# Modulation blocks of layer two at the layer border, first pair's loads ahead of the last down blocks, and another tensor estimate in the interleaving

## The chip, the cores and the metric

One core of a Trainium2 chip runs the whole program. The metric is device time in microseconds (us), the median of three runs. A profiled execution gives the span of the instructions and the trace.

## The reference

One inference step of a two-layer backbone over 640 tokens (128 prompt tokens and 512 sample tokens that use the same weights), width 1024, in float32. Cut to what matters here, a layer is

```
shift1, scale1, gate1, shift2, scale2, gate2 = split(silu(cond) @ w_ada[l] + b_ada[l], 6)   # one vector per group
h = rms_norm(x) * (1 + scale1) + shift1
z = h @ w_in                     # conv streams, q, k, v, state-space input u, three branch gates
merged = sum of three gated branches (conv, attention, bidirectional state space), each through its own projection
x += gate1 * (merged @ w_out)
h = rms_norm(x) * (1 + scale2) + shift2
x += gate2 * ((silu(h @ w_ffn_gate) * (h @ w_ffn_up)) @ w_ffn_down)      # inner width 2816
```

## The kernel before

**Products.** The residual x lives in eight tiles of 128 features by 640 tokens. A float32 product is made of three products of rounded halves (high by high, high by low, low by high), each over 2 x 320 columns; one weight block of 128 output features over 8 feature tiles is 48 products of 320 columns. The feed-forward part (L1966 on) has three plain blocks m = 0, 1, 2 (a gate block and an up block each) and then pairs: from m = 3 a gate and an up block are made together by a scheme of seven products in place of eight (`glu_pair`, L901, 84 products of 320 columns). `sums` (L860) makes the combined activations for it. The 22 inner blocks come in five parts of 4, 4, 4, 5 and 5; each part ends in eight down blocks (m = 0 to 7) that add into x. The part's last block lets the norm of the next stage begin.

**Weights.** `order` lists all weight blocks in the order of their use. `w_fill` (L385) issues the loads in this order on SP's queue into three raw slots (`wr`); a pair takes one `wr` slot and two `pt` tiles, and two of its parts are summed in flight by a second transfer that POOL issues with an add. `converter` (L429) is a side job that turns each raw block into a rounded high half (ScalarE cast) and a low half (VectorE subtraction), up to two blocks ahead of the one in use (`may`, L417). Modulation blocks pass by the converter: `w_get` (L482) takes them raw.

**Modulation.** w_ada is used in blocks of 512 x 256 (512 KB), four products each. `ada_n` (L319) says after which weight block how many modulation blocks come: in the first layer one after every pair (m = 3 to 21), one after most projection blocks, and so on. Those in the gaps are loaded by `ada_pre` (L670) into ordinary `c` tiles and multiplied by `ada_fill` (L682). The norm of the feed-forward part fills its waits with them (`FILL2` = 0, 5, 5: so many ahead of the last statistics product, ahead of and behind the broadcast product in `rstd` and `norm_rows`, L731 to L760). At the border from layer one to two the counts `FILL1` are 0, 0, 0. `ada_flush` starts a side job that turns finished sums into the vectors (`ada_rows`).

**Order of the work.** All engine queues are in order, and the program writes them by an interleaving planner. The main stream (weight blocks) yields what it needs next; `pump` (L534) then steps side jobs (converter, sums, state space, attention) whose next step is due, by a running estimate of each engine's time (`Clock`, `Engine`), no later than the main stream's. The estimate of a product is at L142: (columns + 32) / 2.4 ns, so 146.7 ns for 320 columns; a VectorE operation on 640 columns is taken as 737 ns. `clk.calm` keeps state-space and attention jobs back; it is set for the last two down blocks of layer one and taken back in `norm`. `cvt.hold` keeps the converter from being stepped in pairs, where `advance` steps it by hand. The state-space side jobs of layer two start ahead of the last eight down blocks of layer one (`ssm_begin`).

Of the kernel before, what the change touches and what calls it, by code (L numbers as in the profile page):

```python
# [17 lines left out]
KD = D // 128  # L18
FF = 2816
KF = FF // 128  # L20
DEPTH = 2
# [8 lines left out]
SLACK = 0  # L30
ADA0 = 2
GO = 0
FILL1 = (0, 0, 0)
FILL2 = (0, 5, 5)
GN, GF = sum(FILL2), sum(FILL1)
CV = 0
# [76 lines left out]
class Engine:  # L113
# [5 lines left out]
    def __getattr__(self, op):  # L119
        f, key, clock = getattr(self.eng, op), self.key, self.clock  # L120

        def is_ap(x):
            return hasattr(x, "partition_size")

        def size(x):
            n = 1
            for d in x.shape[1:]:
                n *= d
            return n

        def call(*args, **kw):
            res = f(*args, **kw)  # L132
            out = kw.get("out", args[0] if args else None)
            ins = [x for x in list(args[1:] if "out" not in kw else args) +
                   [v for k, v in kw.items() if k not in ("out", "accum_out")] if is_ap(x)]
            outs = [out.name] + ([kw["accum_out"].name] if "accum_out" in kw else [])
            n = max([size(out)] + [size(x) for x in ins]) if key != "pe" else size(out)
            if key == "pe":
                if op == "transpose":
                    cost = 2 * n / 2.4  # L140
                elif ins[-1].dtype == F32R:
                    cost = (max(n, 256) + 32) / 2.4  # L142
                else:
                    cost = 4 * n / 2.4
                    if out.shape[0] == 32:
                        cost /= 3
            elif key == "act":
                cost = 100 + n / 1.2 + (90 if "accum_out" in kw else 0)
            elif key == "dve":
                one = op in ("tensor_scalar", "tensor_copy", "memset") and all(x.space == out.space for x in ins)  # L150
                cost = 70 + n / (1.6 if one else 0.96)
            else:
                s = max([clock.t["pe"] if key == "dma" else clock.t[key]] + [clock.avail.get(x, 0.0) for x in outs] +
                        [clock.w.get(x.name, 0.0) for x in ins])
                if key == "pool":
                    clock.t[key] = e = s + 1000
                else:
                    clock.issue = max(clock.issue, s) + 475.0
                    rate = 180.0 if min(x.shape[-1] for x in [out] + ins) < 128 else 360.0
                    clock.t[key] = e = max(clock.t[key], clock.issue) + 4 * n * out.shape[0] / rate  # L160
                for x in outs:
                    clock.w[x], clock.by[x] = e + 2000, "dma"
                return res
            clock.op(key, cost, outs, [x.name for x in ins])
            return res
        return call
# [3 lines left out]
def trunk_kernel(ctx: ExitStack, tc: tile.TileContext, a):  # L170
    nc = tc.nc
    clk = Clock()
# [18 lines left out]

    def bps():
        while clk.slot("m") >= clk.HELD:
            min((x for x in sides if not x.busy and not x.hold), key=lambda x: x.time()).step()
        t = psb.tile([128, 2, 512], F32, tag="b", name="bps")
        clk.ring("b", t.name, 4)
        return t
# [121 lines left out]
    def ada_n(key):  # L319

        nm, l, m = key
        if nm == "pa":
            return 1 + int(m == 0)
        if nm == "fgu":
            return int(l == 0)
        if nm == "fd":
            return int(l == 0 and m in (4, 8))
        return int(nm == "o" and m < 7 - GO or l == 0 and (nm in ("cc", "cb") or nm == "fg" and m > 1))
# [50 lines left out]
        ada_gap(GF)  # L379
    assert not ada_o  # L380

    wst = {"load": 0, "use": 0, "made": 0, "used": 0, "over": 0, "pair": 0, "wr": 0, "pt": 0}
    wraw, wtile = {}, {}

    def w_fill():  # L385

        while wst["load"] < len(order):
            key, srcs, nr, ncol = order[wst["load"]]
            part = key[3] if key[0] == "fgu" else 0
            if not part and (wst["wr"] == WR or key[0] == "fgu" and wst["pt"] == 2):  # L390
                return
            if part:
                t = f32(ptp.tile([128, 2, TK], F32R, tag="pt", name="pt").rearrange("p a b -> p (a b)"))
            else:
                t = wrp.tile([128, 1024], F32, tag="wr", name="wr")
                clk.ring("wr", t.name, WR)
                wst["wr"] += 1
                wst["pt"] += int(key[0] == "fgu")
            rows = lambda o, x: (t[:, o:o + x.shape[0] // 128 * ncol].rearrange("p (k m) -> p k m", m=ncol),
                                 x.rearrange("(k p) m -> p k m", p=128))  # L400
            for o, x, y in srcs:
                sp.dma_start(*rows(o, x))
                if y is not None:
                    pool.dma_start(*rows(o, y), accum_op=OP.add)
            wraw[key] = t
            wst["load"] += 1
# [22 lines left out]
    def converter():  # L429
        u = -1  # L430
        raws = []

        def put(hl):
            nonlocal u
            u += 1
            while units[u][0] == "ada":
                u += 1
            wtile[u] = [hl[r].rearrange("p (k m) -> p k m", m=ncol) for r in range(2)]

        for i, (key, srcs, nr, ncol) in enumerate(order):  # L440
            if key[0] == "ada":
                continue
            yield lambda: key in wraw
            raws.append(wraw.pop(key))
            if key[0] == "fgu":
                if key[3] == 2:
                    for hl in pair_units(u + 1, *raws):
                        if not isinstance(hl, list):
                            yield hl
                            continue  # L450
                        put(hl)
                    raws = []
                    w_free("pt")
            else:
                yield may
                put((yield from halves(raws.pop(), nr * ncol)))
                w_free("wr")
# [24 lines left out]
    def w_get(key):  # L482
        u = wst["use"]
        assert units[u] == key, (units[u], key)
        wst["use"] += 1
        if key[0] == "ada":
            return wraw.pop(key)[:, 0:1024].rearrange("p (k m) -> p k m", k=4)
        wst["used"] += 1 - wst["over"]
        wst["over"] = int(key[0] == "fgu" and key[3] == 3)
        while u not in wtile:  # L490
            cvt.step()
        return wtile.pop(u)
# [15 lines left out]
    class Side:  # L508
# [1 line left out]


        def __init__(self, gen, prio):
            self.gen, self.prio, self.done, self.busy, self.hold = gen, prio, False, False, False
            sides.append(self)
            sides.sort(key=lambda x: x.prio)
            self.step()
# [17 lines left out]
    def pump(need=(), until=None):  # L534
# [3 lines left out]
        while until is None or not until.done:  # L538
            if until is not None:
                m = INF  # L540
            elif not own:
                m = max(clk.ready(need), clk.t["pe"])
            t, x = min(((x.time(), x) for x in sides if not x.busy and not x.hold and (x.prio < 0 or not clk.calm)), key=lambda y: y[0], default=(INF, None))
            if t > m + SLACK or x is None or own and t == m and x.prio >= 0:
                return
            assert t < INF
# [101 lines left out]
    def ada_step():  # L648

        if ada["i"] < len(ada_list):  # L650
            w = w_get(("ada",) + ada_list[ada["i"]])
            yield w, "m"
            ada_prod([w[:, k, :] for k in range(4)])
            w_free("wr")
# [92 lines left out]
    def norm_rows(s, fill=(0, 0, 0), after=None):  # L747

        y = yield from rstd(s, fill)
        dg = c2()  # L750
        mul(dg.rearrange("p (i q) -> p i q", i=NT), ident[:, None, :].to_broadcast([128, NT, 128]),
            y[:, :, None].to_broadcast([128, NT, 128]))
# [1137 lines left out]
    def layer(l, xs, stat, ssm):  # L1890
# [2 lines left out]
        yc, merged = [], []  # L1893
        hs = yield from norm(stat, xs, s1T[l], modT[l][:, 0], FILL1 if l else (0, 0, 0))
        spill_x(xs)
        yield from u_project(l, hs, up)
        yield from conv(l, hs, yc)
        if l + 1 < DEPTH:
# [66 lines left out]
        hp = [None] * KD  # L1965
        hs = yield from norm(stat, xs, s2T[l], modT[l][:, 3], FILL2, KS, hp)  # L1966
        tt_ = []
        side = Side(sums(hp, tt_), -0.3)
        ssm = x = None
        for part, (m0, nm) in enumerate(FF_PARTS):  # L1970
            hid = []
            tail = iter([0, 0, 0])
            for m in range(m0, m0 + nm):
                if m >= PLAIN:
                    if x is None:
                        if not side.done:
                            pump(until=side)
                        x = quarters(hs, tt_)
                    cvt.hold = True
                    tail = yield from glu_pair(l, m, x, hid, tail)  # L1980
                    continue
                s = c2()
# [8 lines left out]

                if m == 0:
                    yield from pair_gemm(("fg", l, m), ("fu", l, m), hs, ev_g, ev_u, KS)
                    continue
                yield from tile_gemm(("fg", l, m), hs, ev_g)
                yield from tile_gemm(("fu", l, m), hs, ev_u)
            advance(9)
            for _ in tail:
                pass
            cvt.hold = False  # L2000
            final = m0 + nm == KF
            if not final:
                ada_flush(l, 5)
# [7 lines left out]
            for m in range(KD):  # L2011
# [10 lines left out]
                    w = w_get(("fd", l, m, m0))  # L2022
                    yield from gemm(ps, w, 0, hid)
                if final:
                    clk.calm = m >= KD - 2 and l + 1 < DEPTH
                    if l + 1 < DEPTH and m >= 8 - GF:
                        ada_pre(1)
                    finish_x(m, ps, g2T[l])
                    if l + 1 == DEPTH:
# [135 lines left out]
```

## Time and profile before

| | us |
|---|---|
| median of three runs | 2665.01 (lowest 2661.48, highest 8698.79) |
| profiled execution, its own time | 2660.61 |
| its span | 2658.7 |
| tensor engine busy in it | 2517.6 (95%) |
| vector engine busy | 1831.6 (69%) |
| scalar engine busy | 1163.1 (44%) |
| granted tensor clock, mean | 0.979 |

The 8698.79 is one disturbed run. Products are pipelined, so a product's own duration in the trace (314 ns for 320 columns) overlaps the next one's; the distance between starts is what counts. Times in the rows are us from the start of the span. Layer one's last down block and layer two's first norm lie at about 1349 to 1368; the two feed-forward norms at about 866 to 876 and 2178 to 2188.

### The profile page before, as it was taken

The numbers are of one execution on the slowest core, as the hardware profiler recorded it, in microseconds if no ns is written. First come the engines' busy times: TensorE is split into PE (matmuls) and PEld (weight loads), VectorE is DVE, ScalarE is ACT, GpSimd is POOL, SyncE is SP. The second block draws the span as 40 slices with busy tenths as digits, with TensorE's granted clock in tenths as the row PEclk, the third lists the DMA queues.
The fourth block names the chain that finished last, engine by engine and source line by source line (L and its number), as shares of the span: only waits on it lengthen the run. The fifth ranks groups of instructions, "written<-read, shape, count | busy, mean of one in ns | idle before, by whom it ended". The sixth has DMA issues, their size and how long they took to land. (4 is left out here: it accounts for less than half of the span.)

```text
span 2658.7 us, 45284 instructions
## 1 busy us (share of the span) xinstructions
PE 2517.6 (95%) x18235; PEld 2409.9 (91%) x18235; DVE 1831.6 (69%) x3491; ACT 1163.1 (44%) x2107; POOL 97.9 (4%) x80
## 2 busy tenths in 40 slices
PE   7899999999999999999979999999999999999998
PEld 5889988999999899999978999989999989999998
DVE  5888876788634655665679787667886446666665
ACT  4333336766612433343444333366665234333443
POOL 0000000000000010011000000000000000111010
PEclk8999999999999999999989999999999999999999
DMA  9433321111147365575533233212111552665472
GB/s 264 133 106 96 106 83 44 58 60 51 33 127 242 76 146 121 141 166 139 127 117 98 65 99 103 76 34 66 55 45 36 178 176 60 131 135 116 92 149 70
DMA packets 465202, 280.46 MB, mean 105 GB/s; under 512 B 60184, under 2 KB 453216, under 8 KB 464992
## 3 DMA queue, kind: packets, MB, share of 16 engines
q1 hardware_dynamic: 424864, 257.63, 33.5%
q0 software_dynamic: 40128, 19.93, 6.1%
q8 instruction: 144, 2.36, 0.4%
q14 instruction: 66, 0.54, 0.1%
HBM read 257.37 MB, written 20.12 MB: 104 GB/s over the span
## 5 line engine op out<-in xcount | busy, mean ns | idle before, releaser
L132 PE MATMUL bps<-c,wh 128*128 128x320 f32 x11760 | 1836.3, 314 | 57.9 <-ACT c L132 22.8
L132 PEld LDWEIGHTS bps<-c,wh 128*128 128x128 f32 x11760 | 1754.2, 190 | 98.4 <-ACT c L132 29.0
L132 DVE TENSOR_TENSOR c<-c,c 128x640 f32<-128x640 f32 (+10 forms) x750 | 423.2, 592 | 68.2 <-ACT c L132 58.6
L132 ACT CAST wh<-wr 128x1024 fp32r<-128x1024 f32 (+2 forms) x286 | 267.9, 939 | 356.8 <-PE bps L132 219.8
L132 DVE TENSOR_TENSOR wh<-wr,wh 128x1024 fp32r<-128x1024 f32 (+2 forms) x286 | 309.3, 1087 | 152.4 <-ACT wh L132 150.4
L132 PE MATMUL bps<-c,c 128*128 128x320 f32 (+2 forms) x1416 | 237.1, 305 | 16.2 <-DVE c L132 10.1
L132 ACT COPY c<-bps 128x320 f32<-128x320 f32 (+8 forms) x363 | 150.5, 436 | 214.4 <-PE bps L132 212.2
L132 PEld LDWEIGHTS bps<-c,c 128*128 128x128 f32 x1416 | 205.1, 192 | 23.8 <-ACT c L132 17.3
L132 DVE TENSOR_TENSOR c<-c,bps 128x320 f32<-128x320 f32 (+1 forms) x222 | 125.1, 565 | 132.3 <-ACT c L132 108.6
L132 PE MATMUL bps<-ident,c 128*128 128x128 f32 (+1 forms) x1115 | 163.0, 282 | 30.1 <-DVE c L132 13.7
L132 PE MATMUL bps<-wh,c 128*128 128x256 f32 x1440 | 184.4, 286 | 1.3 <-DVE c L132 1.3
L132 ACT ACTIVATE c<-c 128x640 f32<-128x640 f32 (+4 forms) x131 | 93.5, 722 | 208.1 <-DVE c L132 207.8
L132 PEld LDWEIGHTS bps<-wh,c 128*128 128x128 f32 x1440 | 178.0, 193 | 1.5 <-issue 1.4
L132 PEld LDWEIGHTS bps<-ident,c 128*128 128x128 f32 (+1 forms) x1115 | 130.9, 145 | 47.4 <-issue 17.5
L132 ACT CAST c<-c 128x640 fp32r<-128x640 f32 (+3 forms) x192 | 113.2, 622 | 130.4 <-DVE c L132 120.9
L132 DVE SCALAR_TENSOR_TENSOR c<-bps,g2T,c 128x128 f32<-128x128 f32 (+2 forms) x240 | 89.7, 434 | 84.8 <-PE bps L132 84.8
L132 POOL DMA_DIRECT2D pt<-in_w_ffn_gate_dram x38 | 48.9, 1287 | 2410.4 <-DVE c L132 1919.5
L132 DVE SCALAR_TENSOR_TENSOR c<-c,c 128x640 f32<-128x640 f32 (+3 forms) x124 | 102.8, 836 | 46.8 <-ACT c L132 44.9
L132 ACT ACTIVATE c<-bps,mx 128x640 f32<-128x640 f32 (+1 forms) x160 | 113.2, 712 | 49.2 <-DVE mx L132 48.8
L132 DVE TENSOR_REDUCE mx<-bps 128x1 f32<-128x640 f32 (+1 forms) x136 | 109.8, 809 | 20.6 <-PE bps L132 20.0
L132 ACT CAST wh<-pt 128x1024 fp32r<-128x1024 f32 x76 | 79.2, 1050 | 100.8 <-PE bps L132 50.9
L132 DVE TENSOR_TENSOR pt<-bps,pt 128x640 fp32r<-128x640 f32 (+1 forms) x136 | 109.2, 811 | 16.6 <-ACT pt L132 15.8
(105 smaller groups left out, 1544.6 us busy)
## 6 DMA issues: line engine op xcount, KB each, us to landing
wr<-in_w_in_dram SPq DMA_DIRECT2D x104, 512.0 KB
c<-in_w_ada_dram SPq DMA_DIRECT2D x110, 256.0 KB
wr<-in_w_ffn_gate_dram SPq DMA_DIRECT2D x44, 512.0 KB
wr<-in_w_ada_dram SPq DMA_DIRECT2D x41, 512.0 KB
pt<-in_w_ffn_up_dram SPq DMA_DIRECT2D x38, 512.0 KB
wr<-in_w_ffn_down_dram SPq DMA_DIRECT2D x48, 256.0 KB
wr<-in_w_ffn_down_dram SPq DMA_DIRECT2D x32, 320.0 KB
pt<-in_w_ffn_up_dram SPq DMA_DIRECT2D x38, 256.0 KB
```

What stands on the lines that cost most here:

```text
L132: res = f(*args, **kw)
```

## The change

- `FILL1` becomes 2, 3, 3, so eight modulation blocks are multiplied in the layer border's norm. `ada_n` no longer puts one after the pairs m = 14 to 21, and `ada_pre(1)` loads one in each of layer one's last eight down blocks. An `ada_flush` follows `spill_x` in layer two.
- `w_fill` follows a new list `loads`: the three transfers of the first pair of each part are issued ahead of the last three down blocks' loads (for m = 3, ahead of the two blocks that stand before it).
- The planner's estimate of a product drops the 32 columns (320 columns: 133.3 ns), and its estimate for POOL's transfers rises from 2000 to 4000 ns after the issue.
- Modulation blocks pass through the converter's order and count in its lead of two blocks.
- The hold of the converter is a common flag; it is now also set from down block 6 of the last part until `rstd` is done in the next norm.
- `clk.calm` is set one down block earlier. The side job `sums` starts behind the first plain block instead of ahead of it.

```diff
-FILL1 = (0, 0, 0)
+FILL1 = (2, 3, 3)
...
-                    cost = (max(n, 256) + 32) / 2.4
+                    cost = max(n, 256) / 2.4
...
-                    clock.w[x], clock.by[x] = e + 2000, "dma"
+                    clock.w[x], clock.by[x] = e + (4000 if key == "pool" else 2000), "dma"
...
-            return int(l == 0)
+            return int(l == 0 and m < 14)
...
+    loads = list(order)
+    for i, (key, *_) in enumerate(order):
+        if key[0] == "fgu" and key[3] == 0 and order[i - 1][0][0] != "fgu":
+            j = i - (3 if order[i - 1][0][0] == "fd" else 2)
+            loads[j:i + 3] = order[i:i + 3] + order[j:i]
...
-        while wst["load"] < len(order):
-            key, srcs, nr, ncol = order[wst["load"]]
+        while wst["load"] < len(loads):
+            key, srcs, nr, ncol = loads[wst["load"]]
...
-            if key[0] == "ada":
-                continue
             yield lambda: key in wraw
             raws.append(wraw.pop(key))
-            if key[0] == "fgu":
+            if key[0] == "ada":
+                yield may
+                put([raws.pop()])
+                wst["made"] += 1
+            elif key[0] == "fgu":
...
-        if key[0] == "ada":
-            return wraw.pop(key)[:, 0:1024].rearrange("p (k m) -> p k m", k=4)
...
-            t, x = min(((x.time(), x) for x in sides if not x.busy and not x.hold and (x.prio < 0 or not clk.calm)), key=lambda y: y[0], default=(INF, None))
+            t, x = min(((x.time(), x) for x in sides if not x.busy and not (x.prio == -1 and wst["hold"]) and (x.prio < 0 or not clk.calm)), key=lambda y: y[0], default=(INF, None))
...
         y = yield from rstd(s, fill)
+        wst["hold"] = False
...
         spill_x(xs)
+        if l:
+            ada_flush()
...
-        side = Side(sums(hp, tt_), -0.3)
-        ssm = x = None
+        side = ssm = x = None
...
                     yield from pair_gemm(("fg", l, m), ("fu", l, m), hs, ev_g, ev_u, KS)
+                    side = Side(sums(hp, tt_), -0.3)
                     continue
...
-                    clk.calm = m >= KD - 2 and l + 1 < DEPTH
-                    if l + 1 < DEPTH and m >= 8 - GF:
+                    clk.calm = m >= KD - 3 and l + 1 < DEPTH
+                    wst["hold"] = m >= KD - 2
+                    if l + 1 < DEPTH:
                         ada_pre(1)
```

## Rows read from the trace of the kernel before

**Rows 1.** The page's part 1: busy us (share of the span) and instructions.

```profile
PE 2517.6 (95%) x18235; PEld 2409.9 (91%) x18235; DVE 1831.6 (69%) x3491; ACT 1163.1 (44%) x2107; POOL 97.9 (4%) x80
```

**Rows 2.** Timeline of PE, layer border: start, us, what, count, idle before and releaser.

```profile
1335.88 12.88 PE L132 MATMUL bps<-c,wh 128*128 128x320 f32 x86 [0.52 <-DVE wh L132]
1353.50 4.40 PE L132 MATMUL bps<-ones,c 128*128 128x1 f32 x20 [4.75 <-DVE c L132]
1361.11 2.47 PE L132 MATMUL bps<-c,ones 128*128 128x320 f32 x4 [3.21 <-DVE c L132]
1367.41 18.24 PE L132 MATMUL bps<-c,wh 128*128 128x320 f32 x102 [3.83 <-ACT c L132]
```

**Rows 3.** Timeline of PE, the norm ahead of layer two's feed-forward part.

```profile
2175.81 1.92 PE L132 MATMUL bps<-c,wh 128*128 128x320 f32 x12
...
2188.43 0.56 PE L132 MATMUL bps<-c,wh 128*128 128x320 f32 x2 [1.47 <-ACT c L132]
2189.29 16.18 PE L132 MATMUL bps<-c,wh 128*128 128x320 f32 x98 [0.30 <-DVE c L132]
```

**Rows 4.** Timeline of VectorE, layer border.

```profile
1343.33 4.68 DVE L132 TENSOR_TENSOR c<-c,c 128x512 f32<-128x512 f32 x7
1347.93 1.13 DVE L132 SCALAR_TENSOR_TENSOR c<-bps,g2T,c 128x128 f32<-128x128 f32 x3
...
1354.32 1.22 DVE L132 TENSOR_TENSOR wh<-wr,wh 128x1024 fp32r<-128x1024 f32 x1
```

**Rows 5.** Windows, layer border: us, busy of PE, PEld, DVE, ACT, POOL, clock, DMA.

```profile
1349.00:1368.00 19.00, 7.46 (x26) 6.02 (x26) 13.12 (x43) 6.64 (x10) 0.00 (x0) 0.61 0.33 108
```

**Rows 6.** Timeline of PE, a modulation block between pairs of layer one.

```profile
1282.55 0.64 PE L132 MATMUL bps<-c,csT 128*32 128x256 f32 x8
1283.12 10.82 PE L132 MATMUL bps<-c,wh 128*128 128x320 f32 x72
```

**Rows 7.** Timeline, all engines, layer two, last down blocks ahead of m = 12.

```profile
2353.79 1.28 POOL L132 DMA_DIRECT2D pt<-in_w_ffn_up_dram  x1 [0.64 <-DVE wh L132]
...
2363.11 0.69 DVE L132 TENSOR_TENSOR pt<-pt,wr 128x512 f32<-128x512 f32 x1 [5.53 <-DMA pt<-in_w_ffn_up_dram]
...
2370.24 7.08 PE L132 MATMUL bps<-c,wh 128*128 128x320 f32 x36 [1.87 <-DVE c L132]
```

**Rows 8.** Waits of PE in 940 to 1320 (first row), in 2250 to 2640 (others).

```profile
PE bps L132 <- DVE c L132: 7.8, 5, 1.9
...
PE bps L132 <- DVE c L132: 5.6, 3, 1.9
PE bps L132 <- ACT c L132: 2.5, 3, 1.2
```

**Rows 9.** Timeline, first plain block of layer one's feed-forward part.

```profile
889.55 0.48 DVE L132 TENSOR_TENSOR c<-c 128x320 f32<-128x320 f32 x1
...
894.60 3.49 DVE L132 TENSOR_TENSOR wh<-wr,wh 128x1024 fp32r<-128x1024 f32 x3
...
895.87 4.43 PE L132 MATMUL bps<-c,wh 128*128 128x320 f32 x18 [3.87 <-DVE wh L132]
```

**Rows 10.** Timeline of PE, end of attention, layer one and layer two.

```profile
724.37 10.71 PE L132 MATMUL bps<-c,wh 128*128 128x320 f32 x72
...
2038.80 8.07 PE L132 MATMUL bps<-c,wh 128*128 128x320 f32 x54
```

**Rows 11.** Waits of PE in 62 to 736 (two rows) and in 1388 to 2048.

```profile
PE bps L132 <- DVE c L132: 14.1, 14, 2.2
PE bps L132 <- ACT c L132: 9.1, 13, 2.0
...
PE bps L132 <- DVE c L132: 16.4, 14, 3.3
PE bps L132 <- ACT c L132: 8.7, 13, 1.5
```

**Rows 12.** Windows, attention of layer one: columns as in rows 5.

```profile
395.00:724.00 329.00, 316.60 (x2296) 303.09 (x2296) 249.41 (x467) 215.58 (x435) 0.00 (x0) 1.00 0.16 50
```

More of the change, by code (lines that the diff above doesn't have):

```diff
@@ L193, in bps @@
         while clk.slot("m") >= clk.HELD:
-            min((x for x in sides if not x.busy and not x.hold), key=lambda x: x.time()).step()
+            min((x for x in sides if not x.busy and not (x.prio == -1 and wst["hold"])), key=lambda x: x.time()).step()
         t = psb.tile([128, 2, 512], F32, tag="b", name="bps")
@@ L380, in trunk_kernel @@
     assert not ada_o
-    wst = {"load": 0, "use": 0, "made": 0, "used": 0, "over": 0, "pair": 0, "wr": 0, "pt": 0}
+    loads = list(order)
[3 more added lines that the diff above has]
+            loads[j:i + 3] = order[i:i + 3] + order[j:i]
+    wst = {"load": 0, "use": 0, "made": 0, "used": 0, "over": 0, "pair": 0, "wr": 0, "pt": 0, "hold": False}
     wraw, wtile = {}, {}
     def w_fill():
-        while wst["load"] < len(order):
-            key, srcs, nr, ncol = order[wst["load"]]
+        while wst["load"] < len(loads):
+            key, srcs, nr, ncol = loads[wst["load"]]
             part = key[3] if key[0] == "fgu" else 0
@@ L435, in put @@
             u += 1
-            while units[u][0] == "ada":
-                u += 1
-            wtile[u] = [hl[r].rearrange("p (k m) -> p k m", m=ncol) for r in range(2)]
+            wtile[u] = [x.rearrange("p (k m) -> p k m", m=ncol) for x in hl]
         for i, (key, srcs, nr, ncol) in enumerate(order):
-            if key[0] == "ada":
-                continue
             yield lambda: key in wraw
             raws.append(wraw.pop(key))
-            if key[0] == "fgu":
+            if key[0] == "ada":
[3 more added lines that the diff above has]
+            elif key[0] == "fgu":
                 if key[3] == 2:
@@ L512, in __init__ @@
         def __init__(self, gen, prio):
-            self.gen, self.prio, self.done, self.busy, self.hold = gen, prio, False, False, False
+            self.gen, self.prio, self.done, self.busy = gen, prio, False, False
             sides.append(self)
@@ L650, in ada_step @@
         if ada["i"] < len(ada_list):
-            w = w_get(("ada",) + ada_list[ada["i"]])
+            w, = w_get(("ada",) + ada_list[ada["i"]])
             yield w, "m"
@@ L1978, in layer @@
                         x = quarters(hs, tt_)
-                    cvt.hold = True
+                    wst["hold"] = True
                     tail = yield from glu_pair(l, m, x, hid, tail)
@@ L1999, in layer @@
                 pass
-            cvt.hold = False
+            wst["hold"] = False
             final = m0 + nm == KF
```

## The prediction

> **What bounds the kernel.** I read the page's busy shares first, then the tensor engine's timeline at the stage borders, then who released it. The tensor engine is busy for 95% of the span [rows 1], so a change can only take products off it or close its waits; the other engines matter where they hold it up. Four places show this.
>
> At the layer border the last down product ends at 1335.88 + 12.88 = 1348.76 and the next weight product starts at 1367.41: 18.7 us, with three waits of 4.75, 3.21 and 3.83 us inside [rows 2]. The same chain (last down or output product, square, sum, root, broadcast, scaling) takes 2188.43 - 2177.73 = 10.7 us at layer two's feed-forward norm, where modulation products fill its waits [rows 3]. What is longer at the layer border is the vector queue ahead of the sums: seven state-space operations of 4.68 us end just as the first of three late additions into x starts at 1347.93, and a weight conversion of 1.22 us follows the third [rows 4]. The clock falls too: 0.61 granted in this stretch, a mixture of the 1.2 and the 2.4 GHz level, after the tensor engine had been idle for 4.75 us [rows 5].
>
> Between pairs of layer one a modulation block takes 1283.12 - 1282.55 = 0.57 us of a tensor engine that has nothing to wait for [rows 6].
>
> At the turn from down blocks to the next part's first pair VectorE waits 5.53 us for a summed transfer that POOL issued 9.32 us earlier; the additions and conversions behind it in the queue are late, and the tensor engine stops for up to 1.87 us [rows 7]. Over layer one's inner part these waits are 7.8 us, over layer two's 5.6 + 2.5 [rows 8].
>
> Behind the first plain block the tensor engine waits 3.87 us for the next block's low half, which VectorE makes behind the operations of `sums` that begin at 889.55 and the block's own evaluation [rows 9]; layer two has one more such wait of the same size.
>
> **The change, part by part.** The sum is made against the profiled execution, 2660.61, which is 4.4 under the median of the runs.
>
> *Layer border, fill, hold and calm.* By the border of [rows 3] the chain would be 18.7 - 10.7 = 8.0 us shorter. The first pair of blocks takes 18.24 us behind the border against 17.04 (2188.43 to 2189.29 + 16.18) in [rows 3], both with 100 products or so; 1.2 us of that is the slow clock. So 9.2 at most. At least nothing: calm one block earlier removes steps only behind down block 5's addition, and the seven operations of [rows 4] stand ahead of it; only the lower product estimate (five down blocks of 30 products, 13.3 ns each, is 2.0 us less of planned time) can push that step past the line, where calm then keeps it until the norm. The held conversions of the first two blocks come back behind the root: two subtractions of 1.22 us [rows 4], one beside the broadcast product, one perhaps ahead of the first scaling. I take 9.2 - 1.2 = **-8.0**, nearest to the filled border, because conversion, clock and state-space step all improve in its direction. If the queue stays as late, next is the same 4.75 us wait. The eight blocks themselves fill waits of 11.8 us with 8 x 0.57 = 4.6 us and cost nothing there; with the chain at 10.7 us the cover is still enough, since ten blocks sit in the norm of layer one's feed-forward part and eight in that of [rows 3].
>
> *Eight blocks out of the pairs.* 8 x 0.57 = **-4.6**. Their 16 loads of 256 KB move to the last eight down blocks, on SP's queue between down loads and next layer's blocks; they take `c` tiles that the layer's activations have just left. I cost this at nothing: the converter works two blocks ahead, and that is what hides a load late by one block. Without that cover, each late block would show as a wait of the size in [rows 7].
>
> *First pair's loads.* Three down blocks of 24 products at 0.147 us are 10.6 us. The transfer of [rows 7] would land that much earlier and VectorE waited 5.53, so the wait goes at m = 4, 8 and 12 of both layers. At m = 17, where the down blocks ahead have 30 products, no wait shows in [rows 8] already. All of it is 7.8 + 5.6 + 2.5 = 15.9; the least is nothing, if the down loads pushed back take its place. They lose one of three `wr` slots for about two blocks. I take **-15**, since the two blocks of lead in the converter are 7 us and the pair's first transfers are 1.3 MB.
>
> What speaks against it is a rule of the Trainium skill, DMA: Bandwidth & Descriptors, section Issuing engines are not separate DMA queues: transfers from SP and GpSimd run on the same 16 engines and interleave. By that rule the pair's transfers are paid for by the three down loads behind them, and the sum would lose its 15. The long 9.32 us between issue and release in [rows 7] agrees with shared engines, but says nothing of who is late next.
>
> *`sums` behind the first block.* Its first four vector operations, 0.48 us each, leave the queue ahead of the next block's subtraction [rows 9], and the planner then sees VectorE free at the pair's last yield, so that this subtraction is put ahead of the evaluation. Between nothing and 2 x 3.87; I take **-7**. `sums` is next due at m = 3, some 28 us later (four blocks of 48 products), and VectorE's later conversions cover it.
>
> *Modulation blocks in the converter's lead.* Only where two of them follow one block, behind the first attention projection, does the lead run out: the next block's subtraction then stands behind the evaluation. One subtraction of 1.22 us per layer [rows 4] is shown at most; at least nothing. I take **+2.4** for the two.
>
> *The product estimate.* Products start every (10.71 - 0.31) / 71 = 0.1465 us [rows 10], the old estimate to the letter; the new one is 9.1% short. VectorE's operations run 4.68 / 7 = 0.669 us in [rows 4] where the planner's formula gives 70 + 512 / 0.96 = 603 ns, 11% more. So the old plan orders side work too early against the vector engine, and the tensor engine meets unfinished operands: 14.1 + 9.1 us of waits in layer one and 16.4 + 8.7 in layer two [rows 11]. The new plan has both engines short by about the same. Upper gain: these 48.3 us. Upper loss: attention falls behind its cover. After its last product the main stream still has 72 products (10.6 us) in layer one and 54 (7.9 us) in layer two [rows 10], which is all the slack there is. The two ends are alike in size, so I take **0**.
>
> POOL's longer estimate only delays conversions in the plan that would have waited anyway: 0. The flush in layer two moves an `ada_rows` that ran in the inner part: 0, hidden beside 100 products of the first pair.
>
> Sum: -8.0 - 4.6 - 15 - 7 + 2.4 = -32.2, so 2628.4 for an execution like the profiled one. Against the median's 4.4 above it I give **2630**.
>
> **Rivals.**
> 1. *The new plan removes the side waits.* For it: [rows 11], and the equal shortness of both estimates. Against: part of those waits are drains, which no plan removes. If half of 48.3 goes, 2630 - 24 = 2606.
> 2. *Attention runs out of cover* (the other side). Side steps fall behind by at most 9.1% of the 662 us from 62 to 724, 60 us, less the 10.6 of cover: 49 us, or 0.15 of the attention's 329 us. VectorE alone needs 0.15 x 249.4 = 37 us for that [rows 12]; the tensor engine's own attention products are part of it, so from 0 to 37 per layer. It decides from a lag of 10.6 us, a sixth of the most. At 20 us per layer the time is 2630 + 40 = 2670, slower than before; at the most 2704. Against it: VectorE is busy for only 249.4 of the 329 us, so the side work isn't all bound by that engine.
> 3. *The early loads are paid by the down loads*: 15 comes back, 2645; with a wait of 1.87 in each of six places as well, 2656 [rows 7]. For it: one slot less. Against: the converter's lead. The Trainium skill's section named above speaks for this one.
> 4. *The change at the border doesn't do what it says*: the vector backlog of [rows 4] is untouched and the eight blocks only pad waits that stay. Of the 8.0 then 4.8 is lost: 2635. For it: the step stands ahead of the line where calm begins.
>
> **How the numbers follow.** Forecast, each part within its bounds and the plan within some 12 us either way: 0.50. Rival 1: 0.19. Rival 2: 0.10. Rival 3: 0.13. Rival 4: 0.08. The range takes the forecast, rival 4, most of rival 3 and most of rival 1, and leaves out rival 2 and the tails: 2604 to 2656. About 2% is what a measurement of this kernel can tell from no change, 53.3 us of 2665: faster begins at 2611.7, which needs more than half of rival 1 on top of the sum, or all parts at their upper ends: 0.16. Slower begins at 2718, beyond rival 2's most: 0.03. The rest, 0.81, is within 2%.
>
> **What would show it.** Right: the border from last down product to next weight product near 11 us, with modulation products in it and at most one slice of slow clock; no wait of VectorE for `pt` at the turns, and the sums of [rows 8] under 1 us per layer; fg of m = 1 starting without the 3.87; waits of [rows 11] no larger. Wrong: a wait of ScalarE or VectorE for `in_w_ffn_down` (rival 3); long stretches with few weight products before the attention projection (rival 2); an addition into x that starts several us behind its product at the border (rival 4). The forecast falls if the plan's shift alone is worth more than 25 us either way.

## The result and the profile after

| | before | after |
|---|---|---|
| median, us | 2663.38 | 2592.61 (2589.88 to 2594.07) |
| ratio, 95% interval | | 0.9735 [0.9716, 0.9754] |
| profiled execution | 2660.61 | 2593.81 |
| its span | 2658.7 | 2591.8 |
| granted tensor clock, mean | 0.979 | 0.983 |

Faster by 2.65%, 71 us of the medians and 66.9 us of the spans, where 2630 was forecast and 2604 was the lower end of the range. The table below cuts both profiled executions at the same events: first weight product, attention projection, feed-forward norm's end, layer border's end, and the same in layer two. The number in brackets is the sum of PE's waits over 0.1 us in that stage, counted in the trace.

| stage, us (waits) | before | after | difference | forecast |
|---|---|---|---|---|
| layer one to attention projection | 688.2 (33.4) | 668.8 (20.3) | -19.4 | 0 |
| projections to feed-forward norm | 139.3 (3.2) | 142.9 (5.1) | +3.6 | +1.2 |
| feed-forward part and border | 491.6 (25.9) | 471.5 (10.0) | -20.1 | -23.5 |
| layer two to attention projection | 680.9 (32.5) | 663.2 (24.4) | -17.7 | 0 |
| projections to feed-forward norm | 140.2 (5.1) | 141.3 (5.9) | +1.1 | +1.2 |
| feed-forward part | 454.9 (14.2) | 441.9 (5.0) | -13.0 | -11 |

The forecast's terms are put where they act, those of both layers in the ratio of [rows 8]. The two feed-forward parts came out near them, though by terms that were off in both directions (below). The miss is the two stretches ahead of the attention projections, 37 us, whose only term was the product estimate, taken as 0.

The page's part 1 of after, which answers to [rows 1]:

```profile
PE 2494.3 (96%) x18235; PEld 2398.9 (93%) x18235; DVE 1838.0 (71%) x3502; ACT 1155.5 (45%) x2096; POOL 97.9 (4%) x80
```

The same 18235 products are busy for 23.3 us less, so only 43.6 of the 66.9 us are waits. So a stop costs more than its length here; two estimates for the rest. There are 51 fewer stops of over 20 ns (106 against 157), and the last product of each shows its 0.314 us instead of the 0.147 to the next start: 51 x 0.167 = 8.5 us. The clock that was not granted, 2658.7 x 0.021 = 55.8 us against 2591.8 x 0.017 = 44.1 us, is at most another 11.7. Together that is 20.2 of the 23.3.

**Layer border.** PE's timeline of after, for [rows 2]; then VectorE's, for [rows 4], and the window for [rows 5]:

```profile
1311.03 4.07 PE L132 MATMUL bps<-c,wh 128*128 128x320 f32 x26 [0.30 <-DVE wh L132]
1316.77 1.25 PE L132 MATMUL bps<-ones,c 128*128 128x1 f32 x10 [1.66 <-DVE c L132]
...
1320.63 2.79 PE L132 MATMUL bps<-c,csT 128*32 128x256 f32 x24
1323.92 2.47 PE L132 MATMUL bps<-c,ones 128*128 128x320 f32 x4 [0.50 <-DVE c L132]
1326.32 2.79 PE L132 MATMUL bps<-c,csT 128*32 128x256 f32 x24
1331.54 0.56 PE L132 MATMUL bps<-c,wh 128*128 128x320 f32 x2 [2.43 <-ACT c L132]
```

```profile
1324.83 3.94 DVE L132 TENSOR_TENSOR c<-c,c 128x512 f32<-128x512 f32 x6
...
1328.68 1.54 DVE L132 TENSOR_TENSOR c<-c,bps 128x640 f32<-128x640 f32 x2
```

```profile
1315.00:1334.00 19.00, 14.11 (x99) 8.32 (x99) 13.09 (x28) 6.81 (x11) 0.00 (x0) 0.71 0.67 233
```

The border takes 1331.54 - 1315.10 = 16.4 us, against 18.7 before and about 10.7 forecast. The waits of 4.75, 3.21 and 3.83 became 1.66, 0.50 and 2.43, but the modulation products in them didn't shorten the chain. The state-space operations no longer stand ahead of the sums; six of them, 3.94 us, now stand between the broadcast product (done at 1326.39) and the first scaling (1328.68). The granted clock, 0.71, is still a mixture. The other runs decide how much of this belongs to the fill (behind the sweep, below).

**Inner part.** Waits of PE, first row in 900 to 1290, the others in 2170 to 2560, for [rows 8]; then the issue and the use of the summed transfer at the turn to m = 8, which is also the turn of [rows 7], not that to m = 12; then a wait at m = 3 of layer two:

```profile
PE bps L132 <- DVE c L132: 2.5, 1, 2.5
...
PE bps L132 <- ACT c L132: 2.1, 1, 2.1
PE bps L132 <- DVE wh L132: 1.4, 1, 1.4
```

```profile
2282.65 1.28 POOL L132 DMA_DIRECT2D pt<-in_w_ffn_up_dram  x1 [0.35 <-issue]
...
2298.42 0.69 DVE L132 TENSOR_TENSOR pt<-pt,wr 128x512 f32<-128x512 f32 x1
```

```profile
2185.42 2.65 PE L132 MATMUL bps<-c,wh 128*128 128x320 f32 x12 [2.12 <-ACT c L132]
```

POOL issues the transfer 15.8 us ahead of its use, and VectorE's addition starts with no wait for it. The 2.5 and the 2.1 us are new: both are in m = 3, the second of them in layer two, where the casts of the later `sums` stand before the first pair's copy.

**First plain block,** timelines of PE and VectorE, for [rows 9]:

```profile
860.87 19.35 PE L132 MATMUL bps<-c,wh 128*128 128x320 f32 x125 [0.30 <-DVE c L132]
...
874.00 1.22 DVE L132 TENSOR_TENSOR wh<-wr,wh 128x1024 fp32r<-128x1024 f32 x1
875.57 0.82 DVE L132 SCALAR_TENSOR_TENSOR c<-c,bps 128x640 f32<-128x640 f32 x1 [0.35 <-ACT c L132]
...
878.85 0.48 DVE L132 TENSOR_TENSOR c<-c 128x320 f32<-128x320 f32 x1
```

The subtraction precedes the evaluation and `sums`, and the tensor engine runs on without a stop (the row's 125 products end with its window at 880; in a longer window they are 238): the wait of 3.87 us is gone.

**Attention.** Waits of PE in 62 to 717 (two rows) and in 1352 to 1994, for [rows 11]; then the end of attention in PE's timeline, for [rows 10], and two windows, for [rows 12]:

```profile
PE bps L132 <- ACT c L132: 8.2, 10, 2.8
PE bps L132 <- DVE c L132: 7.5, 12, 1.4
...
PE bps L132 <- DVE c L132: 13.3, 14, 4.2
PE bps L132 <- ACT c L132: 4.8, 7, 1.4
```

```profile
691.01 1.92 PE L132 MATMUL bps<-c,wh 128*128 128x320 f32 x12
...
717.12 0.56 PE L132 MATMUL bps<-c,wh 128*128 128x320 f32 x2 [1.30 <-ACT c L132]
```

```profile
395.00:680.00 285.00, 279.64 (x2012) 274.15 (x2012) 219.58 (x412) 182.00 (x364) 0.00 (x0) 0.98 0.18 54
680.00:717.00 37.00, 31.12 (x215) 28.03 (x213) 27.83 (x55) 26.14 (x59) 0.00 (x0) 0.95 0.00 1
```

Side waits fall from 23.2 to 15.7 and from 25.1 to 18.1 us. Before, 72 weight products were left when attention's last product was done [rows 10]; now the last weight product ends at 692.9 and attention runs alone for 24 us; in the last 37 us ahead of the projection PE is busy for 31.12. So rival 1 and the onset of rival 2 happened together.

### The profile page after: what moved, and what is told of

Same layout as the page of the kernel before. It is cut to its first block, busy times and chain, and to the rows that moved or that the text cites. A ratio compares the mean times of both kernels' runs of the same rounds, so it can differ in the third digit from the quotient of the medians.

```text
span 2591.8 us, 45359 instructions
## 1 busy us (share of the span) xinstructions
PE 2494.3 (96%) x18235; PEld 2398.9 (93%) x18235; DVE 1838.0 (71%) x3502; ACT 1155.5 (45%) x2096; POOL 97.9 (4%) x80
## 5 line engine op out<-in xcount | busy, mean ns | idle before, releaser
L132 DVE TENSOR_TENSOR c<-c,c 128x512 f32<-128x512 f32 (+8 forms) x750 | 423.8, 592 | 57.9 <-ACT c L132 47.8
L132 ACT COPY c<-bps 128x320 f32<-128x320 f32 (+7 forms) x363 | 150.7, 437 | 255.5 <-PE bps L132 250.8
L132 PEld LDWEIGHTS bps<-c,c 128*128 128x128 f32 x1416 | 204.4, 191 | 15.1 <-ACT c L132 10.4
```

## The experiments

Two theories of the estimate stand against each other in them. Proportion (A1): what counts is the ratio of the planner's estimates of PE and of VectorE and ScalarE, and it is best where they are short by the same share. Luck (A3): any other estimate shuffles the order, and this one happens to fall well. The other runs price the change's other parts one by one. Each median is of four or more runs; "before" in the same runs was 2660.74 to 2661.82.

**1. The estimate alone,** in the kernel before.

```diff
-                    cost = (max(n, 256) + 32) / 2.4
+                    cost = max(n, 256) / 2.4
```

> The kernel before with the lower product estimate alone (320 columns: 133.3 ns). Theory A: the estimate makes the 37 us by which the two stretches from the first weight product to the attention projection got shorter (688 to 669 and 681 to 663), so 2663 - 37 = 2626, and the products with few weight blocks at the end of attention appear here too. Theory B, the prediction's zero: the stretches got shorter by other parts of the change (modulation blocks in the converter's lead, the flush), so 2655 to 2668.

Measured: 2637.07, ratio 0.9905 [0.9888, 0.9922], so -25. The two stretches ahead of the projections give 688.2 - 678.5 = 9.7 and 680.9 - 666.5 = 14.4 us, the feed-forward parts nothing (491.6 and 490.0, 454.9 and 456.5). Its waits in 62 to 726:

```profile
PE bps L132 <- DVE c L132: 9.7, 9, 4.7
PE bps L132 <- ACT c L132: 8.3, 10, 2.0
```

18.0 us against 23.2. The term taken as 0 is worth 25 by itself, the very limit at which the prediction says that its forecast falls.

**2. Everything but the estimate:** the changed kernel with the line of 1 turned back.

> The changed kernel with the old product estimate (146.7 ns). Theory A: the 37 us come back in the two stretches, 2593 + 37 = 2630, which is what the prediction gave for the rest of the change. Theory B: 2590 to 2600.

Measured: 2633.31, 0.9891 [0.9871, 0.9911]. This is the forecast's kernel, with the forecast's time: 2630 and 2633. In the changed kernel the estimate is worth 2633.31 - 2592.61 = 40.7 us, more than alone. The first stretch is 690.4 us, with these waits in 62 to 738:

```profile
PE bps L132 <- DVE c L132: 12.8, 15, 2.2
PE bps L132 <- ACT c L132: 10.6, 14, 2.0
```

**3. The other engines' estimates raised** by a tenth in the kernel before, PE's left alone.

```diff
-                cost = 100 + n / 1.2 + (90 if "accum_out" in kw else 0)
+                cost = 1.1 * (100 + n / 1.2 + (90 if "accum_out" in kw else 0))
...
-                cost = 70 + n / (1.6 if one else 0.96)
+                cost = 1.1 * (70 + n / (1.6 if one else 0.96))
```

> The kernel before, old product estimate, with the planner's VectorE and ScalarE estimates raised by a tenth instead. If what counts is the proportion of the two estimates (A1), it gains like the lower product estimate: 2620 to 2640. If what counts is that the plan takes the tensor engine for faster than it is (A2: main work is taken early, whatever the vector engine's estimate), nothing: 2655 to 2670.

Measured: 2636.31, 0.9900 [0.9882, 0.9918]: the gain of run 1, reached from the other side, with 679.4 and 660.6 us in the two stretches. It is the proportion and not the number 133.3. Its waits moved as the theory has it: in layer one's first stretch those ahead of the last 48 weight products fall from 32.0 to 22.5 us, while attention is left without cover for 37.9 us at the end, with 6.7 us of waits there against 1.4. It raises both engines together; which of the two matters is not separated.

**4. The loads ahead alone:** the list `loads` in the kernel before.

```diff
-        while wst["load"] < len(order):
-            key, srcs, nr, ncol = order[wst["load"]]
+        while wst["load"] < len(loads):
+            key, srcs, nr, ncol = loads[wst["load"]]
```

> The kernel before with the first pair's loads ahead of the last down blocks' loads, and nothing else. As predicted: the waits at the turns (7.8 and 8.1 us) go, 2663 - 15 = 2648. Rival 3 (down loads pay for it): 2660 or more, with waits of ScalarE or VectorE for the down blocks' weights.

Measured: 2640.99, 0.9911 [0.9882, 0.994], so -20.8. Waits of PE in its inner part, 940 to 1315, and the turn of layer two:

```profile
PE bps L132 <- DMA c<-in_ssm_c_re_dram: 1.6, 1, 1.6
```

```profile
2324.79 25.39 PE L132 MATMUL bps<-c,wh 128*128 128x320 f32 x172
...
2329.10 1.28 POOL L132 DMA_DIRECT2D pt<-in_w_ffn_up_dram  x1 [0.53 <-DMA pt<-in_w_ffn_up_dram]
...
2335.26 0.62 ACT L132 CAST wh<-wr 128x512 fp32r<-128x512 f32 x1 [5.21 <-DMA wr<-in_w_ffn_down_dram]
...
2345.70 0.68 DVE L132 TENSOR_TENSOR pt<-pt,wr 128x512 f32<-128x512 f32 x1
```

POOL issues 16.6 us ahead of the use instead of 9.32, and the transfer lands 4.4 us after its issue instead of 9.3. The feed-forward parts are 9.7 and 12.0 us shorter, of which 6.9 and 8.2 are waits. The down loads pushed back do come late, the sign that the prediction names for rival 3: ScalarE waits for them nine times, 22.0 us in layer one's feed-forward part and 19.6 in layer two's, and not once before. But the tensor engine runs 172 products on without a stop, as the prediction expected of the converter's two blocks of lead. The one transfer that holds it up is a state-space constant, 1.6 us. The rule weighed against this part (the Trainium skill, DMA: Bandwidth & Descriptors, section Issuing engines are not separate DMA queues) shows none of its price here; whether the down loads are late because of shared engines or because they are issued later on the same queue, the run doesn't tell.

**5. `sums` behind the first block, alone.**

```diff
-        side = Side(sums(hp, tt_), -0.3)
-        ssm = x = None
+        side = ssm = x = None
...
+                    side = Side(sums(hp, tt_), -0.3)
```

> The kernel before with the side job sums started behind the first plain block, and nothing else. As predicted: the two waits of 3.87 us go, 2662 - 7 = 2655, and the second plain block starts without a wait. Rival: the subtraction stays behind the evaluation and the wait stays, 2660 to 2664.

Measured: 2650.75, 0.9957 [0.9944, 0.997], so -10.0 (-8 to -15 by the interval); the feed-forward parts are 5.8 and 3.4 us shorter. PE and VectorE at the first plain block, then PE at m = 3 of layer two:

```profile
880.56 25.62 PE L132 MATMUL bps<-c,wh 128*128 128x320 f32 x168 [0.30 <-DVE c L132]
...
893.67 1.22 DVE L132 TENSOR_TENSOR wh<-wr,wh 128x1024 fp32r<-128x1024 f32 x1
...
2237.54 7.49 PE L132 MATMUL bps<-c,wh 128*128 128x320 f32 x48 [0.87 <-ACT c L132]
```

168 products in a row up to the window's end: the wait behind the first block is gone. At m = 3 the waits are as before, 0.86 and 0.87 us. The 2.5 and 2.1 us of the changed kernel thus come with the lower estimate and not with the late `sums` alone; with the old estimate in these parts (runs 2 and 12) the waits there are 0.86 us again.

**6. The changed kernel without the border's part.**

```diff
-FILL1 = (2, 3, 3)
+FILL1 = (0, 0, 0)
...
-            return int(l == 0 and m < 14)
+            return int(l == 0)
...
-                    clk.calm = m >= KD - 3 and l + 1 < DEPTH
-                    wst["hold"] = m >= KD - 2
-                    if l + 1 < DEPTH:
+                    clk.calm = m >= KD - 2 and l + 1 < DEPTH
+                    if l + 1 < DEPTH and m >= 8 - GF:
```

> The changed kernel without the border part: no modulation blocks at the border (back behind the pairs m = 14 to 21), calm as before, no hold at the border. As predicted, 8.0 + 4.6 us come back: 2593 + 13 = 2605, the border again near 18 us, with its slow clock. Rival: the border was shortened by the lower estimate's smaller vector backlog, and only the blocks' 4.6 come back: 2597.

Measured: 2601.93, 0.9771 [0.9742, 0.98], so the part is worth -9.3; -7.7 of it lies in layer one's feed-forward part and border (479.2 against 471.5). Its border:

```profile
1313.55 4.08 PE L132 MATMUL bps<-c,wh 128*128 128x320 f32 x26 [0.30 <-DVE wh L132]
1321.14 1.44 PE L132 MATMUL bps<-ones,c 128*128 128x1 f32 x10 [3.52 <-DVE c L132]
1328.37 2.47 PE L132 MATMUL bps<-c,ones 128*128 128x320 f32 x4 [3.21 <-DVE c L132]
1334.67 15.50 PE L132 MATMUL bps<-c,wh 128*128 128x320 f32 x89 [3.83 <-ACT c L132]
```

1334.67 - 1317.63 = 17.0 us with empty waits, 16.4 with filled ones. The fill, hold and calm shorten the border by 0.6 us here; that leaves some 7 us of the 7.7 to the eight blocks out of the pairs, an estimate, since the run doesn't separate the two. In layer one's first stretch this program has the same instructions in the same order as the changed one, yet that takes 663.8 against 668.8 us: 5 us is how far one stage scatters between profiled executions. The waits agree (21.3 and 20.3 us); the clock that was not granted there is 3.5 against 11.0 us (stretch times one minus the granted clock).

**7. The changed kernel without the lead:** modulation blocks pass by the converter as before (`w_get` hands them out raw).

> The changed kernel with the modulation blocks passing by the converter, as before. The prediction's step: 2.4 us go, 2590. Theory C, from the stages so far (with the lower estimate alone the first stretch takes 678 us, in the changed kernel 669, and with the old estimate 690): the smaller lead works together with the lower estimate, about 10 us come back in the stretches ahead of the attention projections and 3 to 5 go behind them: 2597 to 2603.

Measured: 2599.35, 0.9764 [0.974, 0.9788]: the lead is worth -6.7, where +2.4 was forecast. Layer one's first stretch is 675.8 against 668.8 us, 5.2 of it waits, layer two's 662.2 against 663.2; behind the projections it costs, as forecast, 142.9 against 141.5 and 141.3 against 139.4.

**8 to 11. The estimate swept in the changed kernel:** `(max(n, 256) + 16) / 2.4` in run 8, -16 in 9, +8 in 10, -8 in 11.

> The changed kernel with the estimate half way, (columns + 16) / 2.4, 140 ns for 320 columns. If the proportion to the vector engine's estimate counts evenly, half of the 41 us between the two estimates: 2612. If attention's lack of cover (about 36 us without enough weight products ahead of each attention projection in the changed kernel) already costs as much as the waits, the half way estimate is as good or better: 2585 to 2600.

> The changed kernel with a still lower estimate, (columns - 16) / 2.4, 126.7 ns for 320 columns. If the proportion counts and 133.3 is where both engines are short alike (A1), going past it uncovers more of attention while few waits are left: 2595 to 2615. If every value of the estimate just draws another order (A3, luck), anything from 2590 to 2635.

> The changed kernel with (columns + 8) / 2.4, 136.7 ns. A1: between the half way estimate (2635) and the changed kernel (2593), 2600 to 2620. A3: no order between the neighbours.

> The changed kernel with (columns - 8) / 2.4, 130 ns. A1: close to the changed kernel, 2590 to 2603. A3: as likely 2610 to 2630.

| estimate for 320 columns, ns | median, us | ratio to before | first stretch, us | last weight product ends before the projection, us | waits earlier / in the last 48 weight products' stretch, us |
|---|---|---|---|---|---|
| 126.7 (9) | 2616.78 | 0.9839 [0.9821, 0.9857] | 675.8 | 68.2 | 13.3 / 16.6 |
| 130.0 (11) | 2604.16 | 0.9790 [0.9771, 0.9807] | 669.1 | 50.8 | 13.2 / 10.6 |
| 133.3 (after) | 2592.61 | 0.9735 [0.9716, 0.9754] | 668.8 | 24.2 | 14.3 / 6.0 |
| 136.7 (10) | 2598.52 | 0.9772 [0.9753, 0.9791] | 677.6 | 15.4 | 24.7 / 4.2 |
| 140.0 (8) | 2634.56 | 0.9894 [0.9869, 0.9918] | 686.8 | 12.7 | 28.6 / 4.6 |
| 146.7 (2) | 2633.31 | 0.9891 [0.9871, 0.9911] | 690.4 | attention ends first | 33.3 / 1.4 |

The times have one bottom, at 133.3, and the last two columns show both slopes in layer one's first stretch. Downwards the earlier waits fall from 33.3 to 14.3 us and then stay; from there on the end of attention, without cover, grows. Layer two's stretch has the same bottom: 672.9, 668.4, 663.2, 665.0, 685.1 and 689.5 us in the order of the table. That layer one's is as short at 130.0 as at 133.3 goes with the clock: 5.8 us of it were not granted there, against 11.0.

Not all of the lower slope is attention. In runs 9 and 11 the wait behind the first plain block is back, in both layers; in layer one of run 11:

```profile
880.02 2.23 PE L132 MATMUL bps<-c,wh 128*128 128x320 f32 x7 [3.85 <-DVE wh L132]
```

The last 80 us of run 9, and waits of run 8 in 62 to 734:

```profile
PE bps L132 <- ACT c L132: 6.5, 10, 1.3
PE bps L132 <- DVE c L132: 5.0, 7, 1.2
PE bps L132 <- DVE pt L132: 4.4, 7, 1.1
```

```profile
PE bps L132 <- DVE c L132: 20.0, 16, 3.6
PE bps L132 <- ACT c L132: 5.9, 9, 1.4
```

In run 9 attention's own chain of engines stops the tensor engine, with nothing to fill in: rival 2. In run 8 it still meets unfinished operands in VectorE's queue. A bottom between two such slopes speaks for proportion; by luck its neighbours, 130.0 and 136.7, had no reason to be better than all that lies further out. At 140.0 the two stretches are 3.6 and 4.4 us shorter than at 146.7, but the stages behind the projections take 3.0 and 2.5 us more and the feed-forward parts 1.4 and 1.6; why, the runs don't say. Run 8 lies outside both of its expected times, and runs 9, 10 and 11 miss the ranges that A1 gave them by 1 to 2 us.

The same runs settle what the border can do. In runs 9, 10 and 11 no state-space operation stands in VectorE's queue around it, and it takes 11.4, 12.5 and 11.9 us; in run 9:

```profile
1319.58 4.08 PE L132 MATMUL bps<-c,wh 128*128 128x320 f32 x26 [0.30 <-DVE wh L132]
...
1335.05 5.14 PE L132 MATMUL bps<-c,wh 128*128 128x320 f32 x22 [0.91 <-ACT c L132]
```

With the same border code but those operations ahead of the sums (run 2) or ahead of the first scaling (runs 7, 8 and 12) it takes 19.2, 18.6, 20.2 and 15.1 us.

**12. An estimate for each stage:** the changed kernel with the old 32 columns in the feed-forward parts alone, where run 2's are shorter (469.6 and 437.2 against 471.5 and 441.9 us).

```diff
-                    cost = max(n, 256) / 2.4
+                    cost = (max(n, 256) + clock.pad) / 2.4
...
+        clk.pad = 32
...
+                clk.pad = 0
```

`pad` starts at 0. The first assignment stands where the feed-forward part begins, the second ahead of the next layer's `ssm_begin`.

> The changed kernel with the lower estimate everywhere but in the inner feed-forward parts, which are ordered by the old one (146.7 ns). By the stages so far those parts took 1.9 and 4.7 us less with the old estimate: 2593 - 6 = 2587. Rival: that was the scatter of a stage from run to run, 2590 to 2595.

Measured: 2584.63 (2584.28 to 2586.72), 0.9717 [0.9702, 0.9732], the fastest of all. Windows of the two feed-forward parts, first of after, then of run 12 (columns as in [rows 5]):

```profile
860.00:1331.00 471.00, 461.48 (x3168) 444.36 (x3168) 314.91 (x549) 192.33 (x292) 48.92 (x38) 0.99 0.58 136
...
2136.00:2578.00 442.00, 437.02 (x2960) 434.64 (x2960) 295.19 (x469) 189.25 (x288) 46.20 (x36) 1.00 0.48 105
```

```profile
860.00:1327.00 467.00, 457.97 (x3168) 443.18 (x3168) 314.89 (x550) 192.42 (x293) 48.93 (x38) 0.99 0.59 138
...
2132.00:2571.00 439.00, 435.48 (x2961) 433.48 (x2961) 294.98 (x469) 189.26 (x288) 46.20 (x36) 1.00 0.48 105
```

4 and 3 us shorter for the same products; the other stages stay within 0.6 us. Of this the border gives 1.4 us (15.1 against 16.4), and the waits of 2.5 and 2.1 us at m = 3 are gone (0.86 is left). So the gain of the estimate belongs to the stretches with attention and state space; in the feed-forward parts it costs some 7 us.

## Why the prediction was wrong

**The step that failed: the product estimate, taken as 0.** The prediction read both sides rightly (old plan early against VectorE by 11%, upper gain the 48.3 us of waits, upper loss the end of cover) and then took 0 because "the two ends are alike in size". That says nothing of the middle, and the likeness wasn't worked out: its own rival 2 puts the loss at 0 to 37 us per layer. The measured value is -25 alone and -40.7 beside the other parts, and run 2, without this step, lies 3 us from the forecast; that is partly luck, since its other terms are off in both directions (below). One thing in the prediction's own rows pointed that way: the proportion, 9.1% and 11%, was nearly equal after the change, and runs 1, 3 and the sweep show that the ratio is what counts. Rival 2's lag, too, goes with PE's estimate against VectorE's and not with PE's against the truth: in run 3 PE's is the old one, and 37.9 us of attention are without cover.

That the best ratio is the one of equal shares is near, but not shown. The 11% come from seven operations of one shape. As an estimate for all 3491 of VectorE in the kernel before, the planner's formulas give 1638 us against 1831.6 busy, 12% more, in line with it. But in layer one's feed-forward part the same reckoning gives 9%, so 133.3 ns should fit there too, and run 12 shows that the old estimate is better there. Why is open.

**Loads ahead, -15:** right in mechanism, -20.8 alone. The waits were sized well (15.1 us gone); 6.6 us more come from what goes with a stop, which the sum left out: as estimates, 11 stops fewer at 0.167 us are 1.8, and 5.0 us less of the clock was not granted in the two parts. Of rival 3 the late down loads came, its price didn't (run 4).

**`sums`, -7:** -10.0 alone. The two waits of 3.87 are gone; what goes beyond their 7.7 us is hardly outside the interval. The waits of 2.5 and 2.1 us at m = 3 belong to this step together with the lower estimate (runs 5 and 12) and stood at nothing in the sum.

**Layer border, -8.0:** mis-sized, -2.3 (18.7 to 16.4). Rival 4 gave -3.2 and is near in size, for another reason: the backlog was touched, but the state-space operations reappeared ahead of the scaling, and the chain of vector and scalar work stayed as long. Run 6 puts only 0.6 us on the fill itself. Judging the filled border by the other norm holds where no such operations are in the queue, 11.4 to 12.5 us in runs 9 to 11, and failed because the changed kernel has six of them there. What puts them there or keeps them out is open. **Eight blocks out of the pairs, -4.6:** not separated; some 7 us by run 6 (-9.3 for the two together).

**Converter's lead, +2.4:** right behind the projections (run 7: 1.4 + 1.9 there), but with the lower estimate the lead gains about 7 us ahead of layer one's first projection, and none in layer two. What the lead is worth with the old estimate was not tried, nor POOL's longer estimate and the flush alone.

The terms, three tried alone and two undone, add up: -24.8 - 20.8 - 10.0 - 9.3 - 6.7 = -71.6, against -70.8 measured. That rests on which were tried alone. With the old estimate all but the estimate gives -28.5 (run 2), and loads and `sums` alone are already -30.8: border, lead and the rest gain nothing there, and 16 us with the lower estimate. So the parts work together, and no single list of prices holds.

## What to carry to other kernels

Where a planner writes the order from estimates, one estimate that equals the hardware is not the aim: here the ratio between the engines' estimates decided, and in the stretches with attention it was best with PE's 9% below the measured distance between starts; in the feed-forward parts the old estimate, at that distance itself, was better. A sweep of one estimate, read stage by stage, shows this. Two bounds of like size are no reason to take zero; ask where between them the two mechanisms balance. When pricing a stop of the tensor engine, add to its length, as an estimate, the pipelined product's end and the clock that is not granted behind it.
